# Second feed-forward entry: 1/z by exp(-ln z) on ScalarE, another order of the first eight products, squares and weight sums moved

## The chip, the cores and the metric

The kernel runs on one core of one Trainium2 chip. A core has TensorE (PE in the profile; PEld is its weight load), VectorE (DVE), ScalarE (ACT), GpSimd (POOL) and SyncE (SP), which run side by side and wait for each other through semaphores. SBUF holds tiles of 128 partitions, PSUM eight banks of 128x512 numbers for PE's results. The metric is the device time of one execution in microseconds; lower is better.

## The reference

A decoder trunk of two layers on x of 1024 positions by 1024 channels, in 32-bit floats. Each layer is a token mixer and a feed-forward network, each behind an RMS norm and added to x:

```
for i in range(DEPTH):                       # DEPTH = 2
    h = rms_norm(x, mix_norm[i])
    x = x + (short_conv_mixer if i == 0 else dilated_attention_mixer)(h, ...)
    h = rms_norm(x, ffn_norm[i])
    x = x + (silu(h @ w_gate[i]) * (h @ w_up[i])) @ w_down[i]     # 1024 -> 2816 -> 1024
return rms_norm(x, final_norm)
```

The attention has 16 heads of 64. For each head three dilated branches are softmaxed and mixed by their log-denominators, which comes to one numerator o and one denominator z for each query; what leaves it is `o / z`, multiplied by `attn_w_out` and added to x.

## The kernel before, in words

Activations are held channel by position: `X[n]`, n = 0 to 7, is a tile of 128 channels by 1024 positions, handled in two halves of 512. Every 32-bit operand is split into a high and a low part, `hi` (a rounded copy, made by ACT, L139 or L556) and `lo` (the rest, made by DVE, L140 or L557), and a product is hi·hi + hi·lo + lo·hi: three matmuls of 128x512 for each 128 rows.

The feed-forward products run as Strassen-Winograd 2x2 block products. A unit u is a pair of weight slabs (even u: gate, odd u: up); it has seven products (u, m), m = 1 to 7, of 12 matmuls each. The right operand `b[m]` is: for m = 1 and 2 the scaled and split first halves of the positions, of channels 0 to 3 and 4 to 7; for m = 6, 7, 4, 5, 3 sums and differences with the second halves. `unit_order` (L258) lists the products in PE's order, and the weights' splits are prepared in the same order by `ensure` and `take`, a few places ahead of PE. `combos` (L187) forms the weights' sums for m = 6, 7, 3 on DVE. Nothing else schedules: each engine executes its instructions in the order in which the program text issues them (a manual schedule), so an instruction that waits holds up all behind it on its engine. All large tiles share one pool of 41 pages; a load waits on SP until its page is free.

The place of the change is the way from attention into the second feed-forward network:

- `slot` and `finish` (L1528) end attention. The last pair of heads (p = 7) is not sent through DRAM: `z` and `o` are copied out of PSUM by ACT (L1523, L1524), DVE forms 1/z by reciprocals of 256 columns (L1555), multiplies (L1549), and o is split into `o_hi`, `o_lo`. Ahead of this last slot, `ensure(ahead_ao)` splits the attention-output weights ("ao", 1, n) up to n = 4; there are eight, n = 0 to 7.
- `by_columns` then multiplies heads' outputs 5 to 7 with these weights: for the first half of the positions (j = 0) n = 0 to 7, then for the second half (j = 1). After each product DVE adds the bank to `X[n]` (L497), ACT squares it (L451, L458) and DVE sums the squares into `acc` (L453), one step late (`put_off`, `flush`).
- `Norm.stats` turns acc into 1/rms: eight matmuls with ones (L476), a root on ACT (L479), a reciprocal and a diagonal matrix on DVE (L480, L485), a matmul with ones (L492) and a copy on ACT (L493) into `rstd`. It runs once for the first half, within j = 1, and once for the second half, within the first products.
- `step` (in `into_ffn`) issues for channel tile k the scaled first half (hcol, L1098), its split into b[1] or b[2], and the gained second half (`gained`, L1120), whose sums run as accumulating DMAs on POOL. `last_step` issues the rest and the last sum of squares.
- `feed_forward` calls `start(n)` after the n-th product of the order: the statistics of the second half, the weight sums, and `second_half` (L1126), which forms the other operands on DVE and ACT, some after each of several products.

Of the kernel before, what the change touches and what calls it, by code (L numbers as in the profile page):

```python
# [17 lines left out]
S = 1024  # L18
# [3 lines left out]
KT = D // 128  # L22
# [73 lines left out]
def trunk(ctx: ExitStack, tc: tile.TileContext, x, gains_in, cwi, ck, cwo, wqkv, wo, relb,  # L96
# [158 lines left out]
        unit[5] = name, lambda: early(op)  # L255
        unit.update({DEEPER + i: (("deep", (key, u), i), lambda i=i: part(i)) for i in WINOGRAD})

    def unit_order(nu, conv):  # L258

        order = [(0, 1), (1, 1), (0, 2), (1, 2), (2, 1), (2, 2), (3, 1)]  # L260
        if conv:
            order += [(3, 2), (4, 1), (4, 2)] + [(u, m) for m in (6, 7, 5, 4, 3) for u in (0, 1)]
            order += [(2, 6), (2, 5), (2, 7)]
        else:
            order += [(3, 2)] + [(u, m) for m in (6, 7, 4, 5, 3) for u in (0, 1)] + [(2, 6), (2, 5), (2, 7)]
        order += [(3, 6), (2, 4), (2, 3), (3, 5), (3, 7)] + [(4, 1)] * (not conv) + [(3, 4), (3, 3)]
        if not conv:
            for u in range(4, SIMPLE):
                order += [(u, 6), (u, 5), (u, 7), (u + 1, 1), (u, 2), (u, 4), (u, 3)]
            for u in range(SIMPLE, nu, 2):  # L270
                order += [(u, 6), (u, 5), (u, 7), (u + 1, 1), (u, 3), (u + 1, 6), (u + 1, 5), (u + 1, 7)]
                deep = [(u + 1, DEEPER + i) for i in DEEP_ORDER]
                order += deep[:4] + [(u + 1, 3), deep[4]] + [(u + 2, 1)] * (u + 2 < nu) + deep[5:]
            return order
        for u in range(4, nu - 1):
            order += [(u, 6), (u, 5), (u, 7), (u + 1, 1), (u + 1, 2), (u, 4), (u, 3)]
        u = nu - 1
        return order + [(u, m) for m in (6, 5, 7, 4, 3)]

    def add_units(key, nu, column):  # L280
# [26 lines left out]
                add_deep(units[u], key, u, [[base + r - 2 * (1 - v) for r in rows] for v in range(2)],  # L307
                         lambda i, u=u: base + 2 * u + {1: 1, 2: 1, 3: 3, 4: 3}.get(i, 2))
        raw_src.extend(slabs[r] for r in range(2 * nu))
        ops.extend(units[u][m] for u, m in unit_order(nu, key == CONV))  # L310

    def add_down(key, w, pairs, chunk, last):

# [218 lines left out]
    class Strassen:  # L532
# [2 lines left out]


        def __init__(self, key, norm, nu, pairs, chunk, tiles, source):
            self.key, self.norm, self.nu, self.order = key, norm, nu, unit_order(nu, key == CONV)
            self.pairs, self.chunk, self.tiles, self.source = pairs, chunk, tiles, source
            self.b = {m: [None] * 4 for m in range(1, 8)}  # L540
            self.parts = {(q, m): dram.tile([128, HALF], F32, name=f"part_{key}_{q}_{m}")
# [545 lines left out]
    class Swiglu(Strassen):  # L1087
# [92 lines left out]
        def feed_forward(self, stats, last_step, after, final=None):  # L1180
            prep = []

            def start(n):
                if n == 0:
                    last_step()
                    for m in (6, 7):
                        combos[self.key, 1](m)
                    ensure(self.at(3, 1))
                elif n == 1:
                    next(stats)  # L1190
                    ensure(self.at(0, 6))
                elif n == 2:
                    run(stats)
                    prep.append(self.second_half())
                    next(prep[0])
                    nc.scalar.activation(scratch, eps, AF.Silu)
                    ensure(self.at(1, 6))
                elif n == 4:
                    ensure(self.at(1, 7))
# [33 lines left out]
    def into_ffn(i, norm):  # L1233
# [12 lines left out]
        def group1(key, ks, acts):  # L1246
# [9 lines left out]
            def between(j, n):  # L1256
# [15 lines left out]
                elif n > begin:  # L1272
                    if n == begin + 1:
                        run(pre.pop())
                        pre.append(sw.first_half())
                    plan = ((0, 1), (2,), (3,), (4,), (5,), (6, 7)) if i else ((0,), (1,), (2, 3), (4,), (5,), (6,), (7,))
                    for k in plan[n - begin - 1]:
                        step(k)

# [27 lines left out]
    def attention(norm):  # L1307
# [219 lines left out]
        def finish(p):  # L1527
# [23 lines left out]
            def parts(h):  # L1551
                split(o[:, half(h)], [t[:, half(h)] for t in acts[p]])

            for c in range(0, S, 256):
                nc.vector.reciprocal(z[:, c:c + 256], z[:, c:c + 256])  # L1555
                scaled(c, c + 256)
                if c % HALF:
                    parts(c // HALF)
                yield

        def attended():
# [96 lines left out]
            next(later, None)  # L1658
        run(later)
        live = {}  # L1660
        ahead_ao = [k for k, f in ops].index(("ao", 1, AO_WIDE - 1))
        for p in range(NPAIR):
            last = p == NPAIR - 1
            if p < NPAIR - 2:
# [218 lines left out]
```

## Time and profile before

| | |
|---|---|
| runs | 2172.75 us median of 3 (2171.66 to 2173.28) |
| the profiled execution's own time | 2172.59 us |
| its span | 2170.8 us, mean granted clock 0.993 |
| PE busy | 2131.4 us (98%) |
| DVE busy | 1735.0 us (80%) |
| ACT busy | 997.3 us (46%) |
| attention-output product, first matmul of n = 3 to the end | from 1481.67 us |
| first product (0, 1) of the second feed-forward network | 1511.94 us |
| product (0, 4) of unit 0 | 1553.43 us |

Times in the profile count from the start of the span. A row of a timeline has start, duration, engine, line, operation, output and inputs, their sizes, how many equal instructions in a row it stands for, and in brackets the idle time ahead of it and what ended that. A matmul's shown duration is longer than the distance to the next, since matmuls are pipelined. A row of a table of stretches has the length, then for PE, PEld, DVE, ACT and POOL the busy time and the number of instructions, the granted TensorE clock (1.00 is full), the share of the 16 transfer engines that is busy, and GB/s.

### The profile page before, as it was taken

To read this page: it belongs to the slowest core of one execution; us is meant where nothing else is said; L and a number is where in the kernel's file an instruction comes from. 1 tells how busy PE (TensorE), PEld (TensorE's weight loads), DVE (VectorE), ACT (ScalarE), POOL (GpSimd) and SP (SyncE) were. 2 spreads that over 40 slices of the span, in tenths; PEclk is the share of its full clock that TensorE was granted. 3 is DMA by queue.
4 is the path that set the end of the run, shared out by engine and by line. 5 is a ranking of instruction groups with operands and counts; after the bars stand their busy time and mean duration, and the time that the engine had idled before them with its cause. 6 is when DMAs were issued, how large, how long until landed. Compare 5 with 4: busy or idle time off the path is not lost.

```text
span 2170.8 us, 30440 instructions
## 1 busy us (share of the span) xinstructions
PE 2131.4 (98%) x11086; PEld 1822.3 (84%) x11086; DVE 1735.0 (80%) x3166; ACT 997.3 (46%) x1792; POOL 172.3 (8%) x224
## 2 busy tenths in 40 slices
PE   8999999999999999999999999999999999999998
PEld 6788877888888878878999999887788888878887
DVE  7798758878888898865777777869988788889886
ACT  7433426444444544445455554535544444454435
POOL 2000001100101000010111111110001001000000
PEclk9999999999999999999999999999999999999999
DMA  7222643313333474323333333544223233365432
GB/s 210 68 93 68 218 146 83 131 69 108 111 107 104 148 266 148 116 61 131 92 92 92 92 92 85 171 127 165 71 88 109 101 108 111 106 235 184 160 93 78
DMA packets 135298, 262.66 MB, mean 121 GB/s; under 512 B 47835, under 2 KB 59115, under 8 KB 135147
## 3 DMA queue, kind: packets, MB, share of 16 engines
q1 hardware_dynamic: 75978, 184.80, 26.6%
q0 software_dynamic: 18000, 52.80, 7.2%
q10 hardware_dynamic: 41168, 23.10, 3.5%
q8 instruction: 88, 1.44, 0.3%
q14 instruction: 64, 0.52, 0.1%
HBM read 187.04 MB, written 66.26 MB: 117 GB/s over the span
## 4 chain that ended last, share of the span: by engine, by line
PE 83%; DVE 8%; ACT 4%; issue 2%; DMA 1%; ACTq 0%; SPq 0%; DVEq 0%
PE bank L564 17%; PE bank L566 17%; PE bank L565 17%; PE bank L362 5%; PE bank L360 5%; PE bank L361 5%; PE bank L1500 4%; PE bank L660 2%; PE bank L659 2%; PE bank L657 2%; PE bank L1428 1%; DVE b L557 1%; PE bank L1427 1%; DVE w L140 1%; DVE x L497 1%
## 5 line engine op out<-in xcount | busy, mean ns | idle before, releaser
L564 PE MATMUL bank<-b,w 128*128 128x512 f32 x1816 | 714.4, 393 | 12.4 <-ACT part L570 6.7
L565 PE MATMUL bank<-b,w 128*128 128x512 f32 x1816 | 711.0, 392 | 0.6 <-DVE b L868 0.6
L566 PE MATMUL bank<-b,w 128*128 128x512 f32 x1816 | 710.2, 391 | 1.1 <-DVE w L140 1.1
L564 PEld LDWEIGHTS bank<-b,w 128*128 128x128 f32 x1816 | 343.6, 189 | 88.1 <-ACT part L570 9.0
L566 PEld LDWEIGHTS bank<-b,w 128*128 128x128 f32 x1816 | 343.0, 189 | 74.0 <-DVE w L140 2.1
L565 PEld LDWEIGHTS bank<-b,w 128*128 128x128 f32 x1816 | 343.6, 189 | 71.5 <-DVE b L868 1.2
L139 ACT ACTIVATE w<-combo 128x512 fp32r<-128x512 f32 (+2 forms) x448 | 229.5, 539 | 266.2 <-DVE combo L187 250.9
L140 DVE TENSOR_TENSOR w<-combo,w 128x512 fp32r<-128x512 f32 (+2 forms) x448 | 254.1, 580 | 44.7 <-ACT w L139 44.3
L570 ACT ACTIVATE part<-bank 128x512 f32<-128x512 f32 x168 | 100.1, 596 | 307.6 <-PE bank L566 303.5
L140 DVE TENSOR_TENSOR w<-raw,w 128x512 fp32r<-128x512 f32 (+2 forms) x312 | 171.6, 568 | 34.4 <-ACT w L139 34.1
L574 DVE TENSOR_TENSOR part<-part,bank 128x256 f32<-128x256 f32 (+1 forms) x328 | 153.9, 497 | 43.5 <-ACT part L570 26.7
L139 ACT ACTIVATE w<-raw 128x512 fp32r<-128x512 f32 (+2 forms) x312 | 151.1, 527 | 45.8 <-PE bank L566 13.4
L787 DVE TENSOR_TENSOR x<-x,bank 128x512 f32<-128x512 f32 x168 | 114.2, 680 | 30.6 <-PE bank L566 30.5
L360 PE MATMUL bank<-w_hi,w 128*128 128x512 f32 (+1 forms) x320 | 120.2, 376 | 1.1 <-ACT w L139 1.1
L362 PE MATMUL bank<-w_hi,w 128*128 128x512 f32 (+1 forms) x320 | 118.7, 371 | 0.7 <-DVE w L140 0.7
L361 PE MATMUL bank<-w_lo,w 128*128 128x512 f32 (+1 forms) x320 | 118.5, 370 | 0.0
L497 DVE TENSOR_TENSOR x<-x,bank 128x512 f32<-128x512 f32 (+1 forms) x104 | 65.9, 641 | 61.0 <-PE bank L362 52.3
L360 PE MATMUL bank<-h_hi,w_hi 128*128 128x512 f32 x256 | 104.6, 408 | 0.3 <-ACT w_hi L139 0.3
L187 DVE TENSOR_TENSOR combo<-raw 128x512 f32<-128x512 f32 (+1 forms) x160 | 102.9, 643 | 0.0
L362 PE MATMUL bank<-h_hi,w_lo 128*128 128x512 f32 x256 | 100.2, 391 | 0.7 <-DVE w_lo L140 0.5
L361 PE MATMUL bank<-h_lo,w_hi 128*128 128x512 f32 x256 | 99.9, 390 | 0.0
L1481 POOL PARTITION_ALL_REDUCE mb<-m x16 | 52.0, 3252 | 422.6 <-DVE m L1478 161.8
(255 smaller groups left out, 3745.9 us busy)
## 6 DMA issues: line engine op xcount, KB each, us to landing
hin<-part SPq DMA_DIRECT2D x126, 256.0 KB
raw<-in_ffn_w_gate SPq DMA_DIRECT2D x44, 512.0 KB
raw<-in_ffn_w_up SPq DMA_DIRECT2D x44, 512.0 KB
part<-sum POOLq DMA_DIRECT2D x72, 256.0 KB, 2.4
raw<-in_ffn_w_down SPq DMA_DIRECT2D x48, 384.0 KB
x<-spill SPq DMA_DIRECT2D x24, 512.0 KB
raw<-in_attn_w_qkv SPq DMA_DIRECT2D x24, 512.0 KB
raw<-in_conv_w_in SPq DMA_DIRECT2D x21, 512.0 KB
```

The source lines that it names most:

```text
L139: nc.scalar.activation(hi, src, AF.Copy)
L140: eng.tensor_tensor(out=lo, in0=src, in1=hi, op=ALU.subtract)
L187: eng.tensor_tensor(out=c, in0=a, in1=b, op=op)
L360: nc.tensor.matmul(b, whi[:, a], ahi[:, s], start=first, stop=False)
L361: nc.tensor.matmul(b, whi[:, a], alo[:, s], start=False, stop=False)
L362: nc.tensor.matmul(b, wlo[:, a], ahi[:, s], start=False, stop=last)
L564: nc.tensor.matmul(b, hi[:, a], bhi, start=start and k == 0, stop=False, skip_group_check=True)
L565: nc.tensor.matmul(b, hi[:, a], blo, start=False, stop=False, skip_group_check=True)
L566: nc.tensor.matmul(b, lo[:, a], bhi, start=False, stop=k == n - 1, skip_group_check=True)
L570: nc.scalar.activation(t, b, AF.Copy)
L574: nc.vector.tensor_tensor(out=t, in0=t, in1=b, op=ALU.add)
L787: nc.vector.tensor_tensor(out=X[n][:, half(h)], in0=X[n][:, half(h)], in1=b, op=ALU.add)
```

## The change

Six edits, which act on the second feed-forward network (key 1) and the end of attention only:

1. `unit_order` takes the key. For key 1 the first seven products are (0,1), (1,1), (2,1), (3,1), (0,2), (1,2), (2,2), operand by operand; before they were (0,1), (1,1), (0,2), (1,2), (2,1), (2,2), (3,1). (3,2) follows in both.
2. `start`: the weight sums of unit 1 come after the first part of the second statistics, not ahead of it. The second part of the statistics, `second_half` and the Silu table follow the fourth product (n = 3), not the third.
3. `between`: at the last tile of j = 1 the sum of its square, which was put off, is issued ahead of the last two `step`s (a flush), not in `last_step`.
4. `finish`: for the last pair 1/z is formed by ACT, in place, as Ln of all 1024 columns and Exp with scale -1 of each half; the four reciprocals go, the products on DVE are of 512 columns.
5. `ahead_ao`: the attention-output weights are split up to n = 6 ahead of the last slot, not up to n = 4.
6. The signatures that pass the key.

```diff
-    def unit_order(nu, conv):
-
+    def unit_order(nu, key):
+
+        conv = key == CONV
         order = [(0, 1), (1, 1), (0, 2), (1, 2), (2, 1), (2, 2), (3, 1)]
...
         else:
+            if key:
+                order = [(u, m) for m in (1, 2) for u in range(4)][:-1]
             order += [(3, 2)] + [(u, m) for m in (6, 7, 4, 5, 3) for u in (0, 1)] + [(2, 6), (2, 5), (2, 7)]
...
             def start(n):
                 if n == 0:
                     last_step()
-                    for m in (6, 7):
-                        combos[self.key, 1](m)
-                    ensure(self.at(3, 1))
+                    if not self.key:
+                        for m in (6, 7):
+                            combos[self.key, 1](m)
+                        ensure(self.at(3, 1))
                 elif n == 1:
                     next(stats)
+                    if self.key:
+                        for m in (6, 7):
+                            combos[self.key, 1](m)
                     ensure(self.at(0, 6))
-                elif n == 2:
+                if n == 2 + self.key:
                     run(stats)
                     prep.append(self.second_half())
                     next(prep[0])
                     nc.scalar.activation(scratch, eps, AF.Silu)
+                if n == 2:
                     ensure(self.at(1, 6))
                 elif n == 4:
                     ensure(self.at(1, 7))
...
                     plan = ((0, 1), (2,), (3,), (4,), (5,), (6, 7)) if i else ((0,), (1,), (2, 3), (4,), (5,), (6,), (7,))
+                    if i and n == KT - 1:
+                        norm.flush()
                     for k in plan[n - begin - 1]:
                         step(k)
...
-            for c in range(0, S, 256):
-                nc.vector.reciprocal(z[:, c:c + 256], z[:, c:c + 256])
-                scaled(c, c + 256)
-                if c % HALF:
-                    parts(c // HALF)
+            nc.scalar.activation(z, z, AF.Ln)
+            for h in range(2):
+                nc.scalar.activation(z[:, half(h)], z[:, half(h)], AF.Exp, scale=-1.0)
+                scaled(h * HALF, h * HALF + HALF)
+                parts(h)
                 yield
...
-        ahead_ao = [k for k, f in ops].index(("ao", 1, AO_WIDE - 1))
+        ahead_ao = [k for k, f in ops].index(("ao", 1, AO_WIDE + 1))
```

The rows below are the instructions in the order in which the engine gets them; L-numbers of the changed kernel are some lines higher, since lines were added.

ACT at the end of attention, before: the splits of the ao weights, the copies of z and o out of PSUM, the high halves of o, and the first square of the next stage.

```order
L139 ACTIVATE w_hi<-oin 128x1024 x2
L139 ACTIVATE w<-raw 128x384 x5
L1523 ACTIVATE z<-bank 64x512
L1524 ACTIVATE o<-bank 64x512
L1523 ACTIVATE z<-bank 64x512
L1524 ACTIVATE o<-bank 64x512
L139 ACTIVATE o_hi<-o 128x512 x2
L458 ACTIVATE acc<-x 128x512
```

ACT at the same place in the changed kernel:

```order
L139 ACTIVATE w<-raw 128x384 x7
L1533 ACTIVATE z<-bank 64x512
L1534 ACTIVATE o<-bank 64x512
L1533 ACTIVATE z<-bank 64x512
L1534 ACTIVATE o<-bank 64x512
L1564 ACT_TABLE_LOAD
L1564 ACTIVATE z<-z 128x1024
L1566 ACT_TABLE_LOAD
L1566 ACTIVATE z<-z 128x512
L139 ACTIVATE o_hi<-o 128x512
L1566 ACTIVATE z<-z 128x512
L139 ACTIVATE o_hi<-o 128x512
```

Two more weight splits stand ahead of the copies, and two table loads, one Ln and two Exp between the copies and the high halves.

DVE from the last two columns of the first half (hcol, with their low halves b) to the products with the second half's 1/rms (x<-x,rstd), before:

```order
L453 TENSOR_TENSOR acc<-acc,sq 128x512
L1098 SCALAR_TENSOR_TENSOR hcol<-x,gains,rstd 128x512
L557 TENSOR_TENSOR b<-hcol,b 128x512
L1098 SCALAR_TENSOR_TENSOR hcol<-x,gains,rstd 128x512
L557 TENSOR_TENSOR b<-hcol,b 128x512 x2
L453 TENSOR_TENSOR acc<-acc,sq 128x512
L187 TENSOR_TENSOR combo<-raw 128x512
L187 TENSOR_TENSOR combo<-combo,raw 128x512
L187 TENSOR_TENSOR combo<-raw 128x512
L140 TENSOR_TENSOR w<-raw,w 128x512
L480 RECIPROCAL r<-r 128x4
L485 TENSOR_TENSOR diag<-eye,r 128x512
```

DVE there in the changed kernel, up to the products with 1/rms:

```order
L456 TENSOR_TENSOR acc<-acc,sq 128x512 x2
L1101 SCALAR_TENSOR_TENSOR hcol<-x,gains,rstd 128x512
L560 TENSOR_TENSOR b<-hcol,b 128x512
L1101 SCALAR_TENSOR_TENSOR hcol<-x,gains,rstd 128x512
L560 TENSOR_TENSOR b<-hcol,b 128x512 x2
L483 RECIPROCAL r<-r 128x4
L488 TENSOR_TENSOR diag<-eye,r 128x512
L187 TENSOR_TENSOR combo<-raw 128x512
L187 TENSOR_TENSOR combo<-combo,raw 128x512
L187 TENSOR_TENSOR combo<-raw 128x512
L140 TENSOR_TENSOR w<-raw,w 128x512 x2
L140 TENSOR_TENSOR w<-combo,w 128x512 x2
```

The last sum of squares stands ahead of the last two columns, and the reciprocal and the diagonal matrix ahead of the weight sums and of all four weight halves; before, two of the weight halves followed the diagonal matrix and the fourth followed the products with 1/rms. On PE the pair of matmuls with the diagonal matrix (L492) stands 12 matmuls later, after the fourth product.

More of the change, by code (lines that the diff above doesn't have):

```diff
@@ L309, in add_units @@
         raw_src.extend(slabs[r] for r in range(2 * nu))
-        ops.extend(units[u][m] for u, m in unit_order(nu, key == CONV))
+        ops.extend(units[u][m] for u, m in unit_order(nu, key))
     def add_down(key, w, pairs, chunk, last):
@@ L537, in __init__ @@
         def __init__(self, key, norm, nu, pairs, chunk, tiles, source):
-            self.key, self.norm, self.nu, self.order = key, norm, nu, unit_order(nu, key == CONV)
+            self.key, self.norm, self.nu, self.order = key, norm, nu, unit_order(nu, key)
             self.pairs, self.chunk, self.tiles, self.source = pairs, chunk, tiles, source
```

## The prediction

> **What bounds the kernel now.** I read the page's busy times first, then the stretches around the second feed-forward entry, then the timelines of the single engines there. On the page the busy times say who is full.
>
> ```profile
> span 2170.8 us, 30440 instructions
> PE 2131.4 (98%) x11086; PEld 1822.3 (84%) x11086; DVE 1735.0 (80%) x3166; ACT 997.3 (46%) x1792; POOL 172.3 (8%) x224
> ```
>
> TensorE (PE) is full for 98% of the span, so only what removes a gap or a slow clock on PE pays. All edits that count act between 1460 and 1560 us. The stretches there (length, then busy time and instructions of PE, PEld, DVE, ACT, POOL, then the granted clock):
>
> ```profile
> 1485.00:1500.00 15.00, 13.95 (x66) 11.13 (x65) 14.12 (x26) 10.47 (x20) 0.00 (x0) 1.00 0.62 222
> 1515.00:1530.00 15.00, 10.99 (x39) 8.55 (x38) 11.17 (x20) 7.88 (x15) 3.37 (x4) 0.77 0.48 107
> 1530.00:1545.00 15.00, 15.00 (x68) 12.39 (x67) 14.90 (x26) 11.40 (x19) 0.00 (x0) 1.00 0.09 19
> 1545.00:1560.00 15.00, 14.44 (x63) 11.41 (x62) 14.90 (x26) 9.39 (x17) 0.00 (x0) 1.00 0.15 52
> ```
>
> PE lacks 1 us in the first row and 4 us in the second, where the clock also falls to 0.77. In the last two rows VectorE (DVE) is as full as PE: 14.90 of 15. On PE's timeline (start, length, the idle time before in brackets) the gaps are:
>
> ```profile
> 1485.52 0.39 PE L362 MATMUL bank<-o_hi,w 128*128 128x512 f32 x1
> 1486.96 0.50 PE L360 MATMUL bank<-w_hi,w 128*128 128x512 f32 x1 [1.05 <-ACT w L139]
> 1488.59 0.40 PE L360 MATMUL bank<-o_hi,w 128*128 128x512 f32 x1
> 1497.44 0.95 PE L476 MATMUL bank<-ones,acc 128*128 128x1 f32 x8
> 1498.24 0.49 PE L360 MATMUL bank<-w_hi,w 128*128 128x512 f32 x1
> ...
> 1517.15 0.39 PE L566 MATMUL bank<-b,w 128*128 128x512 f32 x1
> 1521.55 1.86 PE L476 MATMUL bank<-ones,acc 128*128 128x1 f32 x8 [4.01 <-DVE acc L453]
> 1528.02 1.02 PE L492 MATMUL bank<-diag,ones 128*128 128x512 f32 x2
> ...
> 1553.43 0.50 PE L564 MATMUL bank<-b,w 128*128 128x512 f32 x1
> 1554.72 0.50 PE L566 MATMUL bank<-b,w 128*128 128x512 f32 x1 [0.56 <-DVE w L140]
> ```
>
> An unbroken matmul starts 0.227 us after the one before (15.00 us hold 66 to 68). Gap A, ahead of 1486.96, waits for the split of an attention-output weight: seven starts from 1485.52 to 1488.59 take 3.07 us instead of 1.59, so it costs 1.48. Gap B waits for the last sum of squares; from 1517.15 to 1528.02 are 10.87 us, while at full pace one start (0.23), the eight statistics matmuls (0.80, as from 1497.44 to 1498.24) and twelve more (2.72) need 3.75. Gap B costs 7.12, 2.95 of them through the slow clock. Gap C (0.56) waits for a weight of product (0, 4).
>
> **The change part by part.** *Weights n = 5 and 6 split before the last slot.* The same instructions stand earlier; gap A goes and everything that PE releases there moves forward by 1.48. *Reciprocal to ScalarE (ACT).* Rows of what goes, and of what the new chain is priced by:
>
> ```profile
> 1469.92 1.75 DVE L1555 RECIPROCAL z<-z 128x256 f32<-128x256 f32 x1
> 1459.94 0.61 ACT L1490 ACTIVATE lh<-lh 128x512 f32<-128x512 f32 x1
> 1460.71 1.06 ACT L1490 ACTIVATE ld<-ld 128x1024 f32<-128x1024 f32 x1 [0.16 <-DVE ld L1489]
> 1467.33 0.97 ACT L139 ACTIVATE w<-raw 128x384 fp32r<-128x384 f32 x2 [0.86 <-DMA raw<-in_attn_w_out]
> 1468.33 0.59 ACT L1523 ACTIVATE z<-bank 64x512 f32<-64x512 f32 x1
> 1494.47 0.63 ACT L451 ACTIVATE sq<-x 128x512 f32<-128x512 f32 x1 [0.65 <-DVE x L497]
> 1495.12 1.28 ACT L1266 ACT_TABLE_LOAD   x1
> 1496.42 0.20 ACT L1266 ACTIVATE scratch<-eps 128x1 f32<-128x1 f32 x1
> 1461.09 0.86 SPq L153 DMA_DIRECT2D raw<-in_attn_w_out  x2
> 1466.89 0.33 SPq L153 DMA_DIRECT2D raw<-in_attn_w_out  x1
> part<-sum POOLq DMA_DIRECT2D x72, 256.0 KB, 2.4
> 1479.63 0.39 PE L360 MATMUL bank<-o_hi,w 128*128 128x512 f32 x1
> 1479.86 0.39 PE L361 MATMUL bank<-o_lo,w 128*128 128x512 f32 x1
> ```
>
> DVE loses four reciprocals (6.9 us), but waits for PE's banks there anyway: alone worth nothing. The new chain has to reach PE in time. The load of weight n = 6 is issued at 1466.89; a landing takes 2.4 us (the 256 KB row) to 5.8 us (second load of the pair at 1461.09, issued near 1461.5, split at 1467.33). The transfer engines are little used when it starts, so I take 2.7: split at 1469.6, done 1470.1. Then four copies out of PSUM (2.43, as 1468.33 to 1470.76), table load (1.30 with its gaps), Ln of 1024 columns (1.06, priced as the exponential of 1024), table load (1.30), Exp of a half (0.61), product on DVE (0.68), o_hi (0.63), o_lo (0.69), handovers (0.15): 1478.95. PE wants o_lo at 1479.86. Hidden, with 0.9 us to spare.
>
> The Trainium skill ("ScalarE: Activation LUTs", "What ACT_TABLE_LOAD costs") speaks against this part: about 1.38 us of drain beside the 1.28 of each switch. By it the chain would end near 1481.7, PE would wait 1.85 us, and the sum below would be about 2171.9. The trace shows the 1.28, but 0.02 us before it and 0.02 behind it, so no drain.
>
> *Order of the entry.* On DVE the stretch from the first scaled column to the weight of (0, 4) reads:
>
> ```profile
> 1504.38 1.41 DVE L1098 SCALAR_TENSOR_TENSOR hcol<-x,gains,rstd 128x512 f32<-128x512 f32 x2 [1.18 <-ACT rstd L493]
> 1517.50 0.74 DVE L1098 SCALAR_TENSOR_TENSOR hcol<-x,gains,rstd 128x512 f32<-128x512 f32 x1
> 1520.81 0.68 DVE L453 TENSOR_TENSOR acc<-acc,sq 128x512 f32<-128x512 f32 x1
> 1525.36 0.68 DVE L140 TENSOR_TENSOR w<-combo,w 128x512 fp32r<-128x512 f32 x1
> 1529.71 2.50 DVE L1128 TENSOR_TENSOR x<-x,rstd 128x512 f32<-128x512 f32 x4 [3.67 <-ACT rstd L493]
> 1553.99 1.28 DVE L140 TENSOR_TENSOR w<-raw,w 128x512 fp32r<-128x512 f32 x2
> 1520.08 0.71 ACT L1120 ACTIVATE x<-x,gains 128x512 f32<-128x512 f32 x1
> 1552.28 0.61 ACT L139 ACTIVATE w<-raw 128x512 fp32r<-128x512 f32 x1
> ```
>
> The last square's sum moves ahead of the column started at 1517.50. With the 1.48 of gap A it starts when its square is ready, near 1516.2, and ends at 1516.9; PE has then finished two products at 1515.9 and waits about 1 us instead of 4, too short for the clock to fall (after the 1.05 us of gap A it stayed at 1.00). Gap B's 7.12 shrink to 1. Products (2, 1) and (3, 1), which need the first operand alone, cover the second operand's splits and the 1/rms on its way: the diag is ready near 1522.2, PE asks for it after 24 matmuls, at 1523.2. That wait is hidden with 1 us.
>
> But the work on DVE is not removed, only moved. It runs unbroken from 1504.38 to 1526.04, waits 3.67, and runs unbroken from 1529.71 to the end of the first weight at 1553.99 (1554.67): 24.96 us. In the new order it starts 1.48 earlier, at 1502.90, and is through the splits near 1520.2. There it waits for the root on ACT, behind the last gained column (1519.4 by the row of 1520.08) and two saves: the reciprocal starts near 1521.3, 1.1 us lost. Reciprocal, diag, three sums and four weight halves take 5.1: the rstd products start at 1526.4, 3.3 earlier than before. Of the 24.96 us one weight (0.60) already lies ahead, so the low half of (0, 4)'s weight is ready at 1550.76: **3.9 us earlier than before**.
>
> PE, though, arrives there far earlier: from 1523.2, the diag pair (0.9) and eight products of 2.72, 1545.9 instead of 1553.43. It waits for the high half (row of 1552.28, less 3.9: 1549.0) and then for the low half until 1550.8. Gap C grows from 0.56 to almost 5 us, and most of what gap B gave is waited off there. From this point the order on both engines is as before, so the 3.9 us carry to the end. Against them stands the clock, after a wait of 3.0 us:
>
> ```profile
> 49.72 0.80 PE L564 MATMUL bank<-b,w 128*128 128x512 f32 x1 [2.24 <-ACT part L570]
> 760.32 0.35 PE L657 MATMUL bank<-t,w 128*128 128x256 f32 x1 [2.00 <-DVE part L574]
> 773.19 0.77 PE L564 MATMUL bank<-b,w 128*128 128x512 f32 x1 [3.02 <-ACT b L556]
> 776.61 0.40 PE L566 MATMUL bank<-b,w 128*128 128x512 f32 x1
> ```
>
> After 2.00 us matmuls come at full pace, after 2.24 slow. After 3.02 us eight starts take 3.42 us (773.19 to 776.61) instead of 1.81: 1.6 lost. Bounds: 0 and the 2.95 of gap B. I take 1.2, since two of the eight slow ones lie ahead of the wait for the low half and cost nothing.
>
> Sum: the profiled execution took 2172.59 us; less 3.9, plus 1.2, 2169.9. The median of the runs is 0.16 higher: **2170.0 us**.
>
> **The rivals.**
>
> *PE sets the pace after all* (20%). DVE's waits of about 0.1 us between splits, or work that I count twice, leave DVE earlier by 4 us at (0, 4). Then gaps A, B less 1.05, and C are all won: 1.48 + 6.07 + 0.56 = 8.1, 2164.6. Against it: DVE's 14.90 of 15 us in both stretches.
>
> *DVE sets the pace, the clock holds* (20%). The 3.0 us lie between a gap that kept the clock and one that, like 3.02, lost it. Then 3.9 are won: 2168.8. The Trainium skill ("TensorE: Matmul & The Clock Gate", "What's actually happening") would have it so: the clock falls after an idle window of about 3.4 us. The gap of 2.24 contradicts it as a strict bound.
>
> *The 1/z chain is late* (9%). If the n = 6 load takes 5.8 us, all seven splits and the copies behind them on ACT are 3.1 late, o_lo comes at 1482.05, PE waits 2.2 us at 1479.86 and loses 1.6 to the clock; all else follows PE: 2170.0 + 3.8 = 2173.8, slower than before. It decides from a landing of some 5.7 us. For it: the row at 1467.33 waited for just such a load. Against: that pair shared the transfer engines with a 512 KB load, and a landing beyond 9 us would be needed for more than 0.2%.
>
> *The new wait at (0, 4) eats the rest too* is the upper end of my forecast: clock cost 2.95, 2171.7.
>
> **How the numbers follow.** The forecast holds 48%, from 2168.7 to 2171.7 by the clock's bounds; 3% are unnamed. The range 2165.0 to 2173.0 takes in the forecast, the held clock, half of the case in which PE sets the pace and the start of the late chain. This kernel's measurement tells about 0.2% (4.35 us) from no change: faster means below 2168.4, slower above 2177.1. Faster: the whole of PE's case and 8 of the held clock's 20: 0.28. Slower: the tail of the late chain and part of the unnamed, 0.06. Same: 0.66.
>
> **What would show it.** Right: no idle time on PE near 1486; about 1 us ahead of the second statistics, clock 1.00 there; DVE without a gap over 1.2 us from 1503 to 1550; a wait of PE for ACT, then DVE, at the start of (0, 4), 4 to 5 us in all, followed by slow matmuls. Wrong: PE idle under 2 us there (PE's case), a DVE gap ahead of the rstd products (the root or the diag later than I have it), or PE waiting for o_lo near 1480.

## The result and the profile after

| | before | after |
|---|---|---|
| median of 20 runs | 2172.39 us | 2168.96 us |
| lowest to highest | 2170.58 to 2175.6 | 2167.95 to 2170.5 |
| ratio of the medians, 95% interval | | 0.9984 (0.9978 to 0.999) |
| profiled execution, its own time and span | 2172.59, 2170.8 us | 2170.5, 2168.7 us |

The changed kernel is 3.4 us faster by the medians; the two profiled executions differ by 2.1 us. 2170.0 us was predicted, the median lies 1.0 us lower.

Stretches of the changed kernel (columns as in the prediction):

```profile
1485.00:1500.00 15.00, 15.00 (x68) 11.89 (x67) 14.35 (x24) 9.54 (x17) 0.00 (x0) 1.00 0.34 129
...
1515.00:1530.00 15.00, 14.12 (x64) 11.15 (x63) 13.59 (x24) 11.29 (x22) 2.55 (x3) 1.00 0.40 82
1530.00:1545.00 15.00, 14.57 (x64) 11.75 (x63) 15.00 (x26) 7.61 (x13) 0.00 (x0) 1.00 0.12 36
1545.00:1560.00 15.00, 12.33 (x40) 9.11 (x39) 13.23 (x22) 9.66 (x18) 1.15 (x2) 0.77 0.20 63
```

The microsecond that PE lacked in the first row is there. The clock of 0.77 that stood at 1515 to 1530 stands at 1545 to 1560 now, and PE's hole with it. PE's timeline of the same kernel, from the second statistics to the end of the slow clock:

```profile
1479.35 0.39 PE L363 MATMUL bank<-o_hi,w 128*128 128x512 f32 x1
...
1516.53 1.05 PE L479 MATMUL bank<-ones,acc 128*128 128x1 f32 x8 [0.88 <-DVE acc L456]
...
1523.00 1.02 PE L495 MATMUL bank<-diag,ones 128*128 128x512 f32 x2
...
1540.79 0.50 PE L567 MATMUL bank<-b,w 128*128 128x512 f32 x1 [0.43 <-ACT part L573]
...
1549.12 0.79 PE L567 MATMUL bank<-b,w 128*128 128x512 f32 x1 [2.59 <-ACT part L573]
1549.71 0.63 PE L568 MATMUL bank<-b,w 128*128 128x512 f32 x1
1550.41 0.80 PE L569 MATMUL bank<-b,w 128*128 128x512 f32 x1
...
1555.95 0.40 PE L567 MATMUL bank<-b,w 128*128 128x512 f32 x1
...
1662.99 0.28 PE L660 MATMUL bank<-t,w 128*128 128x256 f32 x1
```

Gap B is 0.88 us, the diagonal matrix is there without a wait, and (0, 4) is what PE waits for: 2.59 us, then a little for the low half. From 1550.41 thirteen starts take 5.54 us where an unbroken pace takes 2.95.

Two rows of this fence serve as marks below. The first o_hi matmul (1479.35) stands behind work that these kernels have in common; it lies between 1477.84 and 1480.98 in fourteen profiled executions, so that spans of single executions can't be compared to better than that. The first matmul of the deep products (`t,w`, 1662.99) lies behind everything that differs. The distance of the two is called **D**: 183.64 us here. In the kernel before it is 185.40:

```profile
1479.63 0.39 PE L360 MATMUL bank<-o_hi,w 128*128 128x512 f32 x1
...
1665.03 0.28 PE L657 MATMUL bank<-t,w 128*128 128x256 f32 x1
```

DVE in the changed kernel, from the low half of o to the low halves of the weight of (0, 4):

```profile
1477.89 0.69 DVE L140 TENSOR_TENSOR o_lo<-o,o_hi 128x512 fp32r<-128x512 f32 x1 [0.70 <-ACT o_hi L139]
...
1480.49 3.08 DVE L500 TENSOR_TENSOR x<-x,bank 128x512 f32<-128x512 f32 x5
...
1502.48 1.41 DVE L1101 SCALAR_TENSOR_TENSOR hcol<-x,gains,rstd 128x512 f32<-128x512 f32 x2 [1.19 <-ACT rstd L496]
...
1520.84 0.18 DVE L483 RECIPROCAL r<-r 128x4 f32<-128x4 f32 x1 [1.04 <-ACT r L482]
...
1526.01 2.49 DVE L1131 TENSOR_TENSOR x<-x,rstd 128x512 f32<-128x512 f32 x4
...
1547.26 2.50 DVE L560 TENSOR_TENSOR b<-hcol,b 128x512 fp32r<-128x512 f32 x4
1549.67 1.29 DVE L140 TENSOR_TENSOR w<-raw,w 128x512 fp32r<-128x512 f32 x2
```

ACT at the end of attention and ahead of (0, 4):

```profile
1472.17 1.28 ACT L1564 ACT_TABLE_LOAD   x1
1473.46 1.06 ACT L1564 ACTIVATE z<-z 128x1024 f32<-128x1024 f32 x1
1474.54 1.28 ACT L1566 ACT_TABLE_LOAD   x1
1475.84 0.63 ACT L1566 ACTIVATE z<-z 128x512 f32<-128x512 f32 x1
...
1545.63 2.43 ACT L559 ACTIVATE b<-hcol 128x512 fp32r<-128x512 f32 x4 [4.41 <-DVE hcol L1131]
...
1548.49 0.58 ACT L573 ACTIVATE part<-bank 128x512 f32<-128x512 f32 x1
```

PE's wait at (0, 4) was ended by the save of product (0, 7) out of its bank (1548.49 to 1549.07), in which (0, 4) is added up. That save stands on ACT behind four high halves of b[5], the operand of (0, 5), which PE wants two products later, and behind one high half of a weight.

### The profile page after: what moved, and what is told of

It is laid out like the page before. It is cut to its first block, busy times and chain, and to the rows that moved or that the text cites. A ratio compares the mean times of both kernels' runs of the same rounds, so it can differ in the third digit from the quotient of the medians.

```text
span 2168.7 us, 30436 instructions
## 1 busy us (share of the span) xinstructions
PE 2131.9 (98%) x11086; PEld 1822.6 (84%) x11086; DVE 1729.5 (80%) x3160; ACT 1002.4 (46%) x1797; POOL 172.3 (8%) x224
## 4 chain that ended last, share of the span: by engine, by line
PE 85%; DVE 7%; ACT 4%; DMA 2%; issue 2%; ACTq 0%; SPq 0%; DVEq 0%
PE bank L567 18%; PE bank L569 18%; PE bank L568 18%; PE bank L365 5%; PE bank L363 5%; PE bank L364 5%; PE bank L1510 4%; PE bank L663 2%; PE bank L662 2%; PE bank L660 2%; PE bank L1438 1%; PE bank L1437 1%; DVE b L560 1%; DVE w L140 1%; PE bank L1378 1%
```

## The experiments

Theory 1 is the prediction's: behind the first scaled column DVE works almost without a gap, and its queue, not PE, sets when (0, 4) and what follows can run. The main rival is that PE sets the pace, so that each gap taken from PE is won. "Slow" counts PE's matmuls of 0.62 or 0.63 us (0.39 at full clock) from 1480 to 1570 us; each costs 0.20. The median of before is that of the runs made beside it.

| kernel | median | of before | ratio (95%) | first o_hi | D | slow |
|---|---|---|---|---|---|---|
| before |  |  |  | 1479.63 | 185.40 | 8 |
| changed | 2168.96 | 2172.39 | 0.9984 (0.9978 to 0.999) | 1479.35 | 183.64 | 11 |
| changed, again | 2169.85 | 2172.31 | 0.9986 (0.9978 to 0.9995) | 1479.43 | 182.76 | 7 |
| b[5] later | 2168.91 | 2172.99 | 0.9983 (0.9974 to 0.9992) | 1478.37 | 181.36 | 0 |
| b[5] and its differences later | 2170.12 | 2172.99 | 0.9986 (0.9978 to 0.9995) | 1478.12 | 183.62 | 11 |
| without edit 3 | 2173.63 | 2172.99 | 1.0001 (0.9992 to 1.001) | 1477.84 | 186.22 | 13 |
| without edit 4 | 2170.88 | 2172.99 | 0.9992 (0.9983 to 1.0) | 1480.00 | 184.06 | 6 |
| b[5] and b[3] later | 2170.34 | 2172.31 | 0.9989 (0.998 to 0.9998) | 1478.08 | 183.00 | 6 |
| differences on GpSimd | 2170.18 | 2172.31 | 0.999 (0.9981 to 0.9999) | 1479.66 | 184.65 | 13 |
| without edits 1 and 2 | 2169.64 | 2172.31 | 0.9986 (0.9977 to 0.9995) | 1479.34 | 182.24 | 7 |
| root's wait filled | 2168.70 | 2172.25 | 0.9983 (0.9974 to 0.9992) | 1478.14 | 180.25 | 0 |
| without edit 5 | 2169.52 | 2172.25 | 0.9989 (0.998 to 0.9998) | 1479.86 | 181.80 | 0 |
| both waits filled, b[5] later | 2166.34 | 2172.25 | 0.9971 (0.9961 to 0.9982) | 1480.04 | 178.99 | 0 |
| before with edits 4 and 5 | 2170.76 | 2172.77 | 0.9988 (0.9979 to 0.9997) | 1480.98 | 182.65 | 7 |

The medians set "without edit 3" apart, and "both waits filled" nearly so: its interval touches that of the changed kernel, its median lies below the lowest of the 20 runs of that. The intervals of the others overlap widely. D is finer, but of one execution each, and it holds the slow clock, which comes and goes (last section). Times "behind the first o_hi matmul" are a row's start less the column of that name.

### The splits of b[5] behind the weight of (0, 4)

```diff
-                elif n in (5, 7, 8, 9, 11):
+                elif n in ((5, 7, 8, 11, 12) if self.key else (5, 7, 8, 9, 11)):
                     next(prep[0], None)
```

> The changed kernel with the splits of the operand of (0, 5) (b[5], four high halves on ACT, four low halves on DVE) issued two products later, behind the halves of the weight of (0, 4); b[3] one product later. Theory 1 (the order of the queues on ACT and DVE sets the start of (0, 4)): the low half of that weight comes four splits (2.4 us) earlier, near 1547.9 instead of 1550.3, the save of (0, 7) is no longer behind four splits on ACT, PE waits 1 to 1.5 us there instead of about 3.3, the clock stays at 1.00 in 1545 to 1560 us, so 2.4 + 2.6 us are won: about 2164 us. Rival 2 (the amount of work on DVE, not its order, sets the pace): the wait goes to the start of (0, 5), where the moved splits are wanted, near 1553: 2168 to 2169 us. Rival 3 (PE waits there for something else, such as a transfer): no change, 2169 us.

PE's waits from (0, 4) on:

```profile
1547.01 0.50 PE L569 MATMUL bank<-b,w 128*128 128x512 f32 x1 [1.03 <-DVE w L140]
...
1555.89 0.50 PE L567 MATMUL bank<-b,w 128*128 128x512 f32 x1 [0.86 <-ACT w L139]
...
1557.62 0.50 PE L569 MATMUL bank<-b,w 128*128 128x512 f32 x1 [1.00 <-DVE w L140]
```

The wait at (0, 4) shrank to 1.03 us, the low half was taken 68.64 us behind the first o_hi matmul instead of 71.06, the clock held: so far theory 1. But 1.86 us of waiting came up at (1, 5), whose weight now stands behind the splits of b[3]. D is 181.36; the changed kernel's 183.64 less eleven slow matmuls (2.2) is 181.4, its second execution's 182.76 less seven (1.4) the same. The new order won nothing but the clock, and the median, 2168.91, shows no more than that. Rival 2 of this run was nearer: the amount of work on DVE sets the pace, its order only distributes the waits.

### The differences for b[5] behind that weight too

```diff
-                elif n in (5, 7, 8, 9, 11):
+                elif n in ((5, 7, 11, 12) if self.key else (5, 7, 8, 9, 11)):
                     next(prep[0], None)
+                    if self.key and n == 11:
+                        next(prep[0])
```

> As the kernel before it in this list, and the four differences that b[5] is made from (2.5 us on DVE) also stand behind the weight of (0, 4), directly ahead of its splits. Theory 1: the weight of (0, 4) is ready near 1546.0, before PE asks for it at 1546.4: no wait there, clock 1.00, third matmul of (0, 4) 3.5 us earlier and 2.6 us of slow clock gone, and the four differences and splits are through near 1551, before PE reaches (0, 5) at 1551.8: about 2163 us. Rival 2 (amount of work on DVE): PE waits 1 to 3 us at (0, 5): 2165 to 2168 us. Rival 3: no change, 2169 us.

```profile
1555.63 0.65 PE L567 MATMUL bank<-b,w 128*128 128x512 f32 x1 [2.19 <-ACT w L139]
...
1557.37 0.79 PE L569 MATMUL bank<-b,w 128*128 128x512 f32 x1 [0.66 <-DVE w L140]
```

No wait at (0, 4), none at (0, 5), and the whole of it, 2.85 us, at (1, 5), in pieces of 2.19 and 0.66 us, with eleven slow matmuls there. D without these is 181.4 again. Theory 1 (2163 us) failed; rival 2 had the wait one product too early, and its 2165 to 2168 us were too low.

### b[3] later as well

```diff
-                elif n in (5, 7, 8, 9, 11):
+                elif n in ((5, 7, 8, 11, 13) if self.key else (5, 7, 8, 9, 11)):
```

> The changed kernel with the splits of b[5] two products later (as in the run of that name) and the splits of b[3] two products later instead of one, behind the halves of the weight of (1, 5), for which PE waited 0.86 and 1.00 us in that run. Theory 1 (DVE works without a gap to the weight of (0, 3), and its queue sets when each weight is ready): the wait at (1, 5) falls under 0.5 us, a wait of about 1.2 us comes up at (0, 3), which starts 1.3 us earlier, the clock stays at 1.00; from the first o_hi matmul to the first of (2, 4) it takes 96.9 us instead of 98.2 and, in the changed kernel, 100.45: 3.5 us faster than the changed kernel beside it, 2165.5 us where that takes 2169. Rival (the moved wait is paid again at (0, 3), since the amount of work on DVE is unchanged): no faster than the run with b[5] alone, 2168.9 us.

```profile
1559.84 0.47 PE L567 MATMUL bank<-b,w 128*128 128x512 f32 x1 [2.33 <-DVE part L577]
```

The wait at (1, 5) went, and 2.33 us came up at (0, 3), which waits for a bank that DVE empties behind the splits of b[3]. D less the slow matmuls is 181.8. Theory 1's number (96.9 us to (2, 4)) was wrong, it took 99.8; the rival of this run was right. The changed kernel beside it took 2169.85, 2.5 us less than the kernel before, not 3.4:

> The changed kernel itself beside the next three, on the same chip. All theories: 2169 us, about 3.4 us less than the kernel before.

### The differences on GpSimd

In `second_half`, with b[5] and b[3] as in the last run:

```diff
-                tt(f[k], h[k], t2[k], ALU.subtract)
+                (nc.gpsimd if self.key else nc.vector).tensor_tensor(out=f[k], in0=h[k], in1=t2[k], op=ALU.subtract)
```

> As the kernel before it, and the four differences that b[5] is made from are formed by GpSimd (POOL), which is idle there, instead of DVE: 2.4 us less work on DVE between 1543 and 1551 us. Theory 1, with DVE's amount of work as the bound: the wait at (0, 4) goes (1.0 us), and (0, 3) starts 1 to 2 us earlier than in the kernel before it: 2164 us. Rival (the difference on GpSimd takes so long, or slows DVE so much, that b[5] is late at (0, 5)): no gain over the kernel before it, or 1 to 3 us slower.

POOL there, and DVE:

```profile
1540.87 10.32 POOL L1161 TENSOR_TENSOR hcol<-x 128x512 f32<-128x512 f32 x4 [19.76 <-DVE x L1131]
```

```profile
1545.45 2.88 DVE L140 TENSOR_TENSOR w<-raw,w 128x512 fp32r<-128x512 f32 x2
1548.96 3.99 DVE L560 TENSOR_TENSOR b<-hcol,b 128x512 fp32r<-128x512 f32 x4 [0.62 <-ACT b L559]
```

The four differences take 10.32 us on POOL instead of 2.50 on DVE: the first 5.22, the others 1.73 to 1.75 each. From 1545.45 on, beside POOL's last 5.7 us, two weight halves take DVE 2.88 us (1.29 in the changed kernel) and four low halves 3.99 (2.50). With the 0.62 us of waiting that is 3.7 us against 2.4 taken off: the rival. Whether less work on DVE would have helped, this run doesn't tell.

### Without edits 1 and 2

The order of the products and `start` as in the kernel before; edits 3, 4 and 5 kept.

```diff
-            if key:
-                order = [(u, m) for m in (1, 2) for u in range(4)][:-1]
...
-                if n == 2 + self.key:
+                elif n == 2:
                     run(stats)
```

> The changed kernel with edits 1 and 2 undone (order of the entry, place of the weight sums and of the second part of the statistics), edits 3, 4 and 5 kept. Theory 1 (DVE's amount of work sets when the weight of (0, 4) is ready, whatever PE does before): PE waits about 3 us for the diagonal matrix or the second operand instead of at (0, 4), and the slow clock comes there: within 1.5 us of the changed kernel, 2169 to 2170.5 us. Rival (the order of the products carries the gain): 2172 us or more.

```profile
1523.20 1.13 PE L493 MATMUL bank<-diag,ones 128*128 128x512 f32 x2 [2.62 <-DVE diag L486]
```

The 2.6 us that the changed kernel waits at (0, 4) stand at the diagonal matrix instead, and seven slow matmuls behind them. D is 182.24, 0.5 less than the changed kernel with as many slow ones (182.76), the median 0.2 us less than that beside it. The order of the entry moved the wait and brought nothing that D or the median shows: theory 1.

### Without edit 3

```diff
-                    if i and n == KT - 1:
-                        norm.flush()
```

> The changed kernel with edit 3 undone: the last sum of squares stands behind the last two columns again. Theory 1 (DVE sets the pace up to (0, 4)): the sum ends near 1519.7 instead of 1516.4, PE waits about 4 us ahead of the second statistics and its clock falls there (6 us lost on PE), but the wait at (0, 4) and the slow clock behind it go in exchange, since DVE is only about 1 us later there: 2169 to 2170 us, within 1 us of the changed kernel. Rival (PE sets the pace, gap B's share of the gain is real): about 6 us slower, 2174 to 2175 us.

PE and DVE of this kernel:

```profile
1518.14 1.16 PE L479 MATMUL bank<-ones,acc 128*128 128x1 f32 x8 [4.01 <-DVE acc L456]
...
1551.06 0.50 PE L567 MATMUL bank<-b,w 128*128 128x512 f32 x1 [2.00 <-ACT part L573]
```

```profile
1527.95 2.50 DVE L1131 TENSOR_TENSOR x<-x,rstd 128x512 f32<-128x512 f32 x4 [2.34 <-ACT rstd L496]
```

Both theories missed: by the ratios to the kernel before it is 1.7 per mille slower than the changed kernel (3.7 us; D 2.6 more), not 0 to 1 us and not 6. The wait came back at 4.01 us as expected, and 2.00 stayed at (0, 4). I had left out that the diagonal pair stands behind 24 matmuls on PE: these are late and slow, the copy of 1/rms is late, and DVE, which had no wait there in the changed kernel, waits 2.34 us. Its first product with 1/rms comes 50.11 us behind the first o_hi matmul instead of 46.66. So DVE sets the pace only as long as PE's pair with the diagonal matrix is in time.

### Without edit 4

Four reciprocals of 256 columns on DVE, as before; the two more weights still split early.

```diff
-            nc.scalar.activation(z, z, AF.Ln)
-            for h in range(2):
-                nc.scalar.activation(z[:, half(h)], z[:, half(h)], AF.Exp, scale=-1.0)
-                scaled(h * HALF, h * HALF + HALF)
-                parts(h)
+            for c in range(0, S, 256):
+                nc.vector.reciprocal(z[:, c:c + 256], z[:, c:c + 256])
+                scaled(c, c + 256)
+                if c % HALF:
+                    parts(c // HALF)
                 yield
```

> The changed kernel with edit 4 undone: 1/z by four reciprocals of 256 columns on DVE again; the attention-output weights still split up to n = 6 ahead of the last slot. Theory 1: o_lo of the first half about 1.2 us later than in the kernel before (two more splits and copies ahead), near 1476.9, 2.6 us before PE wants it; the additions to x are some 3 us later on DVE and catch up before the first scaled column: 2169 us, at most 0.8 more where PE waits for a bank. Rival (the 6.9 us taken from DVE, which sets the pace later, are worth time): 2172 us or more.

```profile
1484.13 1.88 DVE L500 TENSOR_TENSOR x<-x,bank 128x512 f32<-128x512 f32 x3
...
1504.46 1.41 DVE L1101 SCALAR_TENSOR_TENSOR hcol<-x,gains,rstd 128x512 f32<-128x512 f32 x2 [1.19 <-ACT rstd L496]
```

```profile
1500.80 1.12 PE L495 MATMUL bank<-diag,ones 128*128 128x512 f32 x2 [0.98 <-DVE diag L488]
```

The last reciprocal ends at 1482.3, and five additions to x are done 6.0 us behind the first o_hi matmul (1486.01) instead of 4.2 (1483.57 in the changed kernel). DVE doesn't catch up: PE waits 0.98 us for the first diagonal matrix, and the first scaled column comes 24.46 us behind that mark instead of 23.13. Product (0, 1) starts 32.01 us behind it (before: 32.31, changed: 30.68). So edit 4 is worth 1.33 us next to edit 5; D shows 1.5 (182.9 against 181.4 without the slow matmuls). The 0 to 0.8 that I expected was too little.

### Without edit 5

```diff
-        ahead_ao = [k for k, f in ops].index(("ao", 1, AO_WIDE + 1))
+        ahead_ao = [k for k, f in ops].index(("ao", 1, AO_WIDE - 1))
```

> The changed kernel with edit 5 undone: attention-output weights split up to n = 4 ahead of the last slot. The prediction took 1.48 us for this edit: gap A (PE waiting for the split of n = 5) back, the first scaled column and all of DVE behind it 1.5 us later, so 184.3 to 185 us from the first o_hi matmul to the deep products instead of 182.8 to 183.6: 2170.5 us. Rival (edit 4, which starts the additions to x 2 us earlier on DVE and so the squares on ACT, ahead of which the split waited, has taken gap A away already): no gap over 0.3 us near 1486 and no change, 2169 us.

PE where gap A was, and ACT ahead of it:

```profile
1485.98 0.48 PE L363 MATMUL bank<-w_hi,w 128*128 128x512 f32 x1
1486.29 0.39 PE L364 MATMUL bank<-w_lo,w 128*128 128x512 f32 x1
1486.55 0.50 PE L365 MATMUL bank<-w_hi,w 128*128 128x512 f32 x1
```

```profile
1484.86 0.63 ACT L454 ACTIVATE sq<-x 128x512 f32<-128x512 f32 x1 [1.41 <-DVE x L500]
...
1485.40 1.86 ACT L139 ACTIVATE w<-raw 128x384 fp32r<-128x384 f32 x4
```

Gap A doesn't come back: starts are 0.31, 0.26 and 0.34 apart instead of 0.23. The split of n = 5 stands behind squares that wait for DVE's additions, and without the reciprocals the additions are early. Product (0, 1) starts 31.04 us behind the first o_hi matmul, 0.36 later than with edit 5. The rival holds: of the 1.63 us that product (0, 1) gained, edit 4 alone brings 1.27 (32.31 less 31.04), edit 5 alone 0.30 (32.31 less 32.01); edits 1 to 3 don't move this start, as the next run shows (30.67 without them, 30.68 with them).

### Edits 4 and 5 alone

The kernel before with these two:

```diff
-            for c in range(0, S, 256):
-                nc.vector.reciprocal(z[:, c:c + 256], z[:, c:c + 256])
...
+            nc.scalar.activation(z, z, AF.Ln)
...
-        ahead_ao = [k for k, f in ops].index(("ao", 1, AO_WIDE - 1))
+        ahead_ao = [k for k, f in ops].index(("ao", 1, AO_WIDE + 1))
```

> The kernel before with edits 4 and 5 alone (1/z by Ln and Exp, weights split up to n = 6). Counted from the first o_hi matmul to the first matmul of the deep products: 185.40 us in the kernel before. Theory 1 (both engines get past attention 1.6 us earlier, everything behind is as before, gap B with its slow clock and the wait of DVE for 1/rms included): 183.8 us, within 1 us of it by the length of the slow clock, gap B 4.0 us; about 2170.8 us in all. Rival (edits 4 and 5 carry the whole gain of the change, the entry's edits 1 to 3 nothing): 182.8 us, 2169.5 us.

```profile
1521.28 1.05 PE L476 MATMUL bank<-ones,acc 128*128 128x1 f32 x8 [4.03 <-DVE acc L453]
...
1553.33 0.50 PE L566 MATMUL bank<-b,w 128*128 128x512 f32 x1 [0.56 <-DVE w L140]
```

Gap B is there in full, 4.03 us, and still D is 182.65, that of the changed kernel's second execution. Product (0, 1) starts 30.67 us behind the first o_hi matmul. Of the 2.75 us that D lost, 1.64 are won there; the rest is a shorter spell of slow clock behind gap B (here the statistics took 1.05 us at full clock, before 1.86). By D the rival is nearer: these two edits make the gain, and what edits 1 to 3 add can't be seen beside the clock. By the median theory 1 is: 2170.76 us, 2.0 less than the kernel before, where the changed kernel was 3.4 and 2.5 less. The intervals overlap, so whether edits 1 to 3 add nothing or up to 1.4 us isn't settled.

The row of 1553.33 takes the low half of (0, 4)'s weight 72.35 us behind the first o_hi matmul. The kernel before takes it at 75.09, the changed kernel at 71.06, so edits 1 to 3 do bring it 1.29 us earlier; but here nothing is slow behind it, and there seven or eleven matmuls are.

### The root's wait filled

DVE idled 1.04 us for the root. The three weight sums, which wait for nothing, stand ahead of the reciprocal here:

```diff
-                    next(stats)
                     if self.key:
                         for m in (6, 7):
                             combos[self.key, 1](m)
+                    next(stats)
```

> The changed kernel with the three weight sums of unit 1 ahead of the reciprocal and the diagonal matrix on DVE instead of behind them, so that DVE works while it waited 1.04 us for the root on ACT. Counted from the first o_hi matmul to the first matmul of the deep products (t, w), from where all kernels are the same: 183.64 and 182.76 us in two executions of the changed kernel, which differ by the length of the slow clock behind the wait at (0, 4). Theory 1 (DVE works without a gap from the root to (0, 4), so that what it idles ahead is lost for the end): 1.0 us less on DVE, 181.8 with a short and 182.6 with a long stretch of slow clock; the diagonal matrix is ready near 1522.7, PE asks for it at 1523.0. About 2168 us where the changed kernel takes 2169. Rival (the wait is hidden): no change; or PE waits for the diagonal matrix and loses what is won.

```profile
1546.77 0.50 PE L567 MATMUL bank<-b,w 128*128 128x512 f32 x1 [2.15 <-ACT part L573]
...
1548.06 0.50 PE L569 MATMUL bank<-b,w 128*128 128x512 f32 x1 [0.56 <-DVE w L140]
```

The low half is taken 69.92 us behind the first o_hi matmul instead of 71.06: 1.14 earlier, for 1.04 us of filled idle time. D is 180.25 with no slow matmul, 1.15 less than the 181.4 of the changed kernel without them. By D, what DVE idles ahead of (0, 4) is lost for the end: theory 1. The profiled execution is the fastest of eleven (2166.05 us), and the median, 2168.70, doesn't show the microsecond: about 2168 was expected.

### Both waits of DVE filled

On top of that the copy of the first half's 1/rms is issued ahead of the square on ACT that waits for DVE's addition (DVE waited 1.19 us for the copy), and b[5] and b[3] are split later as in the first run of this section, where the clock held behind the smaller waits. The edit for the copy:

```diff
                 elif j and n < 2:
                     ensure(first_op + n + 4)
+                if i and j and n == begin + 1:
+                    run(pre.pop())
...
-                        run(pre.pop())
+                        if not i:
+                            run(pre.pop())
                         pre.append(sw.first_half())
```

> Three moves on top of the changed kernel: the weight sums ahead of the reciprocal (as in the first run of this list), the copy of the first half's 1/rms on ACT and its matmul's issue ahead of the square and the addition of that channel tile (DVE waits 1.19 us for that copy, ahead of the first scaled column), and the splits of b[5] two and of b[3] one product later (no wait over 1.1 us in the run of that name, clock 1.00, 181.36 us from the first o_hi matmul to the deep products). Theory 1 (DVE's work, without a gap, sets the pace): 181.36 - 1.04 - 1.19 = 179.1 us, clock 1.00 from 1485 to 1575 us, 2166 to 2167 us in all. Rival (one of the two waits was hidden or another wait comes up): 180.2 to 181.4 us, 2168 to 2169 us.

```profile
1500.00:1515.00 15.00, 15.00 (x67) 12.21 (x66) 14.93 (x25) 11.25 (x19) 1.01 (x2) 1.00 0.31 102
...
1545.00:1560.00 15.00, 12.62 (x53) 9.23 (x52) 14.76 (x26) 8.90 (x17) 1.68 (x3) 1.00 0.47 158
```

D was forecast at 179.1 and is 178.99. DVE's timeline shows no wait left from 1495 to 1530 us, PE's none from 1500 to 1545. What remains is 2.4 us in three pieces: PE waits for DVE at (0, 4) (0.54) and at (1, 5) (1.01), and there for ACT, too (0.83). This version beats both kernels: 2166.34 us, 0.9971 of before (0.9961 to 0.9982).

## Why the prediction was right, and where it was not

- **The total** was right for its own main reason: gap B was won on PE and waited off again at (0, 4), because DVE's work was moved and not removed. The low half of (0, 4)'s weight was taken 4.31 us earlier than in the profile before (1550.41 against 1554.72), of which 0.28 lie ahead of the first o_hi matmul: 4.03, where 3.9 was forecast. Of these, 1.63 lie ahead of product (0, 1) and 2.40 behind it (1.48 and 2.4 forecast).
- **Gap A costs 1.48 and goes through edit 5, edit 4 alone is worth nothing: this step failed.** The size was right (product (0, 1) came 1.63 us earlier), the edit wrong. "DVE waits for PE's banks there anyway" overlooked that the reciprocals kept the additions to x waiting on DVE, and through the squares the weight's split on ACT. Edit 4 alone brings 1.27, edit 5 alone 0.30.
- **The 1/z chain is hidden with 0.9 us to spare**: right. o_lo ended at 1478.58, PE took it at 1479.58, 1.0 us later. The Trainium skill's drain of about 1.38 us ("ScalarE: Activation LUTs", "What ACT_TABLE_LOAD costs") doesn't show here: between the copy, the two loads and the two functions no start is more than 0.03 us behind the end before it, and the loads take 1.28 us.
- **Gap B shrinks to about 1 us, clock 1.00, the diagonal matrix hidden**: right (0.88 us, 1.00, no wait at 1523.00). That the clock holds behind such a wait isn't certain: of ten executions with 0.87 to 0.92 us there it held in nine and fell in one, the run with the differences on GpSimd (0.89).
- **DVE loses 1.1 us for the root and starts the rstd products at 1526.4**: right (1.04; 1526.01, with the 0.28 1526.29).
- **PE waits at (0, 4) for the high half, then the low half**: the time was right (1549.0 forecast, 1549.12), the first releaser wrong. It was the save of (0, 7), held up on ACT by the splits of b[5]; the 0.43 us at (0, 7), of the same kind, was not foreseen. The wait was shorter than the 4 to 5 us forecast: 2.67 us in all here, 3.15 in the second execution.
- **From (0, 4) on the 3.9 us carry to the end, less 1.2 for the clock.** They carry: from the low half's matmul to the deep products PE takes 110.31 us in the kernel before (1554.72 to 1665.03) and 110.30 to 110.34 in the three other executions that have the same order from there on and whose clock held (without edit 5, root's wait filled, edits 4 and 5 alone). The clock's term was mis-sized for the profiled execution: 112.58 us, so 2.27, near the upper bound of 2.95, which leaves 1.76 of the 4.03, the whole difference of D. In the second execution it was 1.39 (1550.49 to 1662.19), in "without edit 5" nothing, each behind the same wait. The profiled execution therefore lies 0.6 us above its sum of 2169.9 and the median 1.0 us below 2170.0. By the medians the term would be about 0.6 and 1.6 us (4.03 less the 3.43 and the 2.46 gained), which is an estimate; what the clock costs on the mean of all runs can't be read from single traces.
- **"After 2.00 us matmuls come at full pace, after 2.24 slow".** Such a border isn't there. In the same trace PE waits 2.00 us ahead of 1935.63, and seven slow matmuls start at 1937.23; behind the 2.24 us near 50 us none is slow in the changed kernel's second execution. The bounds of the clock's term (0 and 2.95) held; the 1.2 within them rests on the single row at 773.19.
- **The rivals.** PE does not set the pace: three orders that shortened the wait at (0, 4) or took it away met the rest again at (1, 5) or (0, 3). That the clock holds happens in some executions (without edit 5, root's wait filled). What the prediction didn't see is that little of what the first three edits gain on DVE reaches the end: by D, without 1 and 2 nothing is lost (182.24 against 182.76), and edits 4 and 5 alone come to 182.65. With them the slow spell stands behind gap B, with all six edits behind (0, 4), where it costs 1.39 to 2.27. Edit 3 is needed in the new order, where D is 2.6 us longer without it; in the old one it is 182.65 without and 182.24 with it.

## What to carry to other kernels

Where a second engine is full behind a gap, closing the gap on the first engine only moves the wait; look for the second engine's own idle rows ahead of the place, since each microsecond filled there came out at the end (2.2 us filled, 2.4 us less D). Price an edit on an engine that "waits anyway" through all that queues behind it on that engine and, by its products, on the next. When single executions differ by more than an edit is worth, compare the distance of two marks that stand around the edit, and count the slow matmuls in it.

## What was unexpected of the hardware

The clock's fall is not a matter of the wait's length alone. Behind the same wait of 2.6 us at (0, 4) three executions with the same code there went three ways. The changed kernel's first is shown at the top (1549.12 and 1549.71). PE in its second execution, and then in the kernel without edit 5:

```profile
1549.19 0.50 PE L567 MATMUL bank<-b,w 128*128 128x512 f32 x1 [2.59 <-ACT part L573]
1549.53 0.40 PE L568 MATMUL bank<-b,w 128*128 128x512 f32 x1
...
1551.17 0.63 PE L568 MATMUL bank<-b,w 128*128 128x512 f32 x1
```

```profile
1550.02 0.50 PE L567 MATMUL bank<-b,w 128*128 128x512 f32 x1 [2.60 <-ACT part L573]
1550.36 0.40 PE L568 MATMUL bank<-b,w 128*128 128x512 f32 x1
```

Slow at once for 11 matmuls, slow two microseconds later for 7, not slow at all. A wait of 0.89 us was followed by a slow spell from 1519.15 in one run of ten, and the 2.24 us wait near 50 us by one in the changed kernel's first execution and by none in its second. In the kernel before, a spell from 957.7 shows no wait ahead of it, only eight small matmuls (33x512) that took 2.59 us (954.48). The Trainium skill ("TensorE: Matmul & The Clock Gate", "What's actually happening") has a window of about 3.4 us that runs freely, whatever the kernel does, so that the moment of a change depends on where in it the work falls. That fits a spell that varies from execution to execution; the Trainium skill's condition that a whole window was idle does not fit waits of 0.89 to 2.6 us. Most slow spells had 5 to 8 matmuls (1.0 to 1.6 us lost), a few 10 to 12. What starts them was not settled: no run here varied a wait alone.

Three subtractions of 128x512 on GpSimd took 1.73 to 1.75 us each, 0.69 on DVE; the first of the four shows 5.22. Beside the first 4.6 us of that row DVE's instructions kept their 0.68 or 0.69 us. Beside the rest, from 1545.45 to 1551.19, two weight halves and two low halves on DVE took 1.09 to 1.77 us each instead of 0.69, and the next low half, from 1551.66 on, 0.68 again.
